# Low halves of the weights, the last norm's factors and v's copies: which engine does them in the second block

## The chip, the cores and the metric

The kernel runs on one core of a Trainium2 chip. The metric is the device time of one execution in microseconds (us). A core has five engines that run side by side, each through its own queue in order: TensorE (PE in the rows; PEld is its loading of weights), VectorE (DVE), ScalarE (ACT), GpSimd (POOL) and SyncE (SP, which here only issues the transfers from HBM).

## The reference

Two blocks on 256 tokens of width 1024. The first is two hybrid attention layers with an MLP and a norm at the end; the second is one layer with a modulation, two mixers and 16 experts. What matters here:

```python
x = first_block(...)                       # ends in rms_norm(x, norm_final)
h_l = modulate(rmsnorm(x, norm1), sh1, sc1)      # latents
h_c = modulate(rmsnorm(ctx, norm1), sh1c, sc1c)  # context
# mixer: both through w_in (columns for q, kv, rope, x_m, z and two gates)
x_c = silu(dwconv(x_m, conv_w, conv_b))          # five taps
q, k, v = blockdiag(x_c, w_q), blockdiag(x_c, w_k), blockdiag(x_m, w_v)
# MLA attention of the latents over context and latents, and an mLSTM over both
x = x + g1 * ((sigmoid(g_mla) * y_mla + sigmoid(g_ml) * y_ml) @ w_out)
x = x + g2 * ec_moe(modulate(rmsnorm(x, norm2), sh2, sc2))   # 16 experts, 201 MB of weights
return rmsnorm(x, final_norm)
```

## The kernel before

Activations lie with features on partitions: `xT` is 8 tiles of 128 features by 256 tokens. A float32 product is made of three fast ones (`three`): both operands are split into a high half (the value rounded to float32r) and a low half (what the rounding leaves), and high times high, high times low and low times high are summed in PSUM. Weights come by `load_w` into four buffers `wr` and are split piece by piece in the generator `pieces` (512 columns each): ScalarE casts the high half (`A.copy`, L352), then `src - high` gives the low half, on VectorE (L358) or, for the share of pieces that `share[0]` sets, on GpSimd (L356). In the second block there are four places for pieces, so ScalarE and VectorE can be up to four pieces ahead of TensorE; a piece of a `w_stationary` product is 12 matmuls of 256 columns.

TensorE's order is written out by hand in the program. The other engines' orders are made by the scheduler of the framework when the program is built, from the dependences and the priorities that the code gives (`tc.high_priority`); each engine then runs its queue in that order, and an instruction that waits holds up all behind it.

The first block and its second MLP end near 771 us of the profiled execution. The second block then goes through these stages:

- **Context** (771 to 842 us). Four products `xm`, then the features (`ml_features`): per feature tile k, `conv` makes `pre` (one operation on ScalarE, L1125, four scalar_tensor_tensor on VectorE, L1127), its tanh `cth` on ScalarE and `xcc` on VectorE (L1131). `products(f)` for f = 0, 2, 4, 6 makes v (`per_token`, eight matmuls into `bd`, copied by L1160 into `vex`) and k (`per_feature`, from `xcc`, copied by ScalarE, L1164, into `kT`), and the gates. The tiles `bd` of v come from the pool `accp` with two banks, of which the gates' sum `og` holds one, so v's product for f + 2 waits for the copy of f. Beside it run keys and values of the context (`keys_values`: `kvl`, `kn`, `v`), the norm at the end of the first block and the latents' modulation (`modt`, L975, and `hx`, L981 and L982).
- **Latents** (842 to 889 us): the same features for the latents (`xh` is their `xc`).
- **mLSTM** (889 to 960 us), with gate products (`tanh`) between its steps.
- **Readout, keys, values and queries of the latents** (960 to 1012 us).
- **Attention and output product** (1012 to 1108 us).
- **Routing and experts** (1108 us to the end). Expert weights are loaded into buffers that the stages before leave free, in one queue on SP.

`share[0]` was set to 0.34 in the context and latents stages and to 0.2 after them (`SH1`, `SH2`, `SH3`); in the second MLP it is 0.2 (`SHM`) and the MLP leaves it at `SH0`, which is 0.

The norm at the end of the first block isn't applied to `xT` at once: its factors (gain `g_fin` per feature, `rb1` per token) go into the modulation, and at the end of the context stage `xT` itself is multiplied by both, in two operations for each k:

```python
for k in range(8):
    A.activation(xT[:, k], xT[:, k], AF.Copy, scale=vc("g_fin", k))     # L1660
    G.tensor_tensor(xT[:, k], xT[:, k], rb1, op=OP.mult)                # L1661
```

Of the kernel before, what the change touches and what calls it, by code (L numbers as in the profile page):

```python
# [10 lines left out]
AF = mybir.ActivationFunctionType  # L11
OP = mybir.AluOpType
# [32 lines left out]
TAIL = 4  # L45
HP = 40
SH0 = 0.0
SH1 = (0.34, 0.34, 0.34)
SH2 = 0.34
SH3 = 0.2  # L50
NG = 1
FX = (2.0, 5.0, 1.0, 4.0)
FL = 2.0
# [188 lines left out]
def fused_kernel(ctx: ExitStack, tc: tile.TileContext, I, out):  # L242
    nc = tc.nc
    V, A, G, PE = nc.vector, nc.scalar, nc.gpsimd, nc.tensor
# [24 lines left out]
    xT = per.tile([128, 8, 256], FT, name="xT")  # L269
# [17 lines left out]
    def vc(n, j=0, w=1):  # L287
        o = vcols[n][0] + j
        return vbuf[:, o:o + w]
# [35 lines left out]
    share = [0.0, 0.0]  # L325
# [790 lines left out]
    def ml_features(xs, xc, kT, vex, gp, wg, tp):  # L1116


        xm = tp.tile([128, 8, 260], FT, tag="xm", name="xm")
        V.memset(xm[:, :, 0:2], 0.0)  # L1120
        V.memset(xm[:, :, 258:260], 0.0)
        def conv(j):
            for k in (2 * j, 2 * j + 1):
                pre = tp.tile([128, 256], FT, tag="pre", name="pre", bufs=2)
                A.activation(pre, xm[:, k, 0:256], AF.Identity, scale=vc("cw", k), bias=vc("cb", k))  # L1125
                for w in range(1, 5):
                    V.scalar_tensor_tensor(pre, xm[:, k, w:w + 256], vc("cw", w * 8 + k), pre, op0=OP.mult,  # L1127
                                           op1=OP.add)
                th = tp.tile([128, 256], FT, tag="cth", name="cth", bufs=2)
                A.activation(th, pre, AF.Tanh, scale=0.5)  # L1130
                V.scalar_tensor_tensor(xc[:, k], th, 1.0, pre, op0=OP.add, op1=OP.mult)  # L1131

        for j in range(4):
            o = fl_tile("xm")
            yield from w_stationary(load_w(I["w_in2"][j]), xs, o)
            A.copy(xm[:, 2 * j:2 * j + 2, 2:258], pair(o))
            if CV[j] is not None:
                conv(CV[j])
            yield None
        og = acc_tile("gt")  # L1140

        def per_token(o, n, src, f):
            for j in range(2):
                b = bds[:, 8 * n + f + j]
                for t in range(2):
                    c0 = t * 256 + j * 128
                    mm(o[:, c0:c0 + 128], src[:, f + j, t * 128:(t + 1) * 128], b, j == 0 and t == 0, True)

        def per_feature(o, n, f):
            for j in range(2):  # L1150
                mm(o[:, j * 256:(j + 1) * 256], bds[:, 8 * n + f + j], xc[:, f + j], j == 0, True)

        def tokens(o):
            return o[:, 0:512].rearrange("p (t n) -> p t n", t=2)

        def products(f):
            o = acc_tile("bd")
            per_token(o, 0, xm[:, :, 2:258], f)
            with tc.high_priority(offset=HQ):
                V.tensor_copy(vex[:, :, f // 2], tokens(o))  # L1160
            o = fl_tile("bd")
            per_feature(o, 1, f)
            with tc.high_priority(offset=HQ):
                A.activation(kT[:, f:f + 2], pair(o), AF.Copy, scale=1.0 / 64)  # L1164
            for j in range(2):
                for i, rhs in enumerate((xc[:, f + j], xm[:, f + j, 2:258])):
                    g = 2 * j + i
                    mm(og[32 * g:32 * g + 32, 0:256], wg[:, i * 8 + f + j], rhs, f == 0, f == 6)

        for f in (0, 2, 4, 6):  # L1170
            products(f)
            if CV[4 + f // 2] is not None:
                conv(CV[4 + f // 2])
            yield 2.6
            yield None
        A.copy(gp[-1], og[:, 0:256])
# [419 lines left out]
    vex = [mx_.tile([128, 2, 4, 256], FT, name=f"vex{s}") for s in range(2)]  # L1596
# [7 lines left out]
    with ExitStack() as es:  # L1604
        fp = pool(es, "b2c")
        xcc = fp.tile([128, 8, 256], FT, name="xcc")

        def ctx_path():
            yield from in_turn(ml_features(cx, xcc, kTc, vex[0], gp, wg, fp),
                               keys_values(0, cx, kn[0], vt[0], kp0, fp))  # L1610

        share[0] = SH1[0]
        cg = F.add(ctx_path())

        s1 = fp.tile([128, 256], FT, name="s1")
        s2 = fp.tile([128, 256], FT, name="s2")
        for k in updated(dn):
            for s_, sc, eng in ((s1, 1.0, G), (s2, vc("g_fin", k), V)):
                d = s_ if k == 0 else fp.tile([128, 256], FT, tag="sqf", name="sq", bufs=3)
                A.activation(d, xT[:, k], AF.Square, scale=sc)  # L1620
                if k:
                    eng.tensor_tensor(s_, s_, d, op=OP.add)
            F.fill(FX[2])
        share[0] = SH1[1]
        scg = fp.tile([128, 32], FT, name="scg")[:, 0:8]
        V.tensor_tensor(scg, sc1[:, 0], vc("g_fin", 0, 8), op=OP.mult)
        F.fill(FX[0])
        r1 = rstd_cols(s1, 1024, "fin")
        ps = acc_tile("ps_s2")
        for t in range(2):  # L1630
            mm(ps[:, t:t + 1], s2[:, t * 128:(t + 1) * 128], ones[:, 0:1], t == 0, True)
        r2 = fp.tile([128, 2], FT, name="r2")
        V.scalar_tensor_tensor(r2, ps[:, 0:2], 1.0 / 1024, r1, op0=OP.mult, op1=OP.mult)
        V.tensor_tensor(r2, r2, r1, op=OP.mult)
        V.tensor_scalar(r2, r2, EPS, None, op0=OP.add)
        G.tensor_tensor(r2, r2, mhalf[:, 0:2], op=OP.pow)
        V.tensor_tensor(r2, r2, r1, op=OP.mult)
        F.fill(FX[1])
        rb2 = fp.tile([128, 256], FT, name="rb2")
        bcast_rows(r2, rb2)  # L1640
        rb1 = fp.tile([128, 256], FT, name="rb1")
        bcast_rows(r1, rb1)
        for _ in modulated(xT, rb2, scg, modT[:, 0, 0:8], fp, into(hh, hl)):
            F.fill(FX[3])
        share[0] = SH1[2]
        F.need(cg)

        sh2 = modT[:, 0, 24:32]
        ss = per.tile([128, 8], FT, name="ssh")
        lb0 = per.tile([128, 16], FT, name="lb0")  # L1650
        lb_ps = fl_tile("lb0")
        sw = fp.tile([128, 8, 16], FT, name="sw")
        V.tensor_tensor(sw, vc("wrt", 0, 128).rearrange("p (k e) -> p k e", k=8),
                        sh2[:, :, None].to_broadcast([128, 8, 16]), op=OP.mult)
        sws = fp.tile([128, 16], FT, name="sws")
        V.tensor_reduce(sws, sw.rearrange("p k e -> p e k"), axis=AX.X, op=OP.add)
        mm(lb_ps[:, 0:16], ones, sws, True, True)
        V.tensor_copy(lb0, lb_ps[:, 0:16])
        for k in range(8):
            A.activation(xT[:, k], xT[:, k], AF.Copy, scale=vc("g_fin", k))  # L1660
            G.tensor_tensor(xT[:, k], xT[:, k], rb1, op=OP.mult)  # L1661
    xh_ = x2p.tile([128, 2, 2048], FT, tag="xh", name="xh")
    xc = xh_[:, 0].rearrange("p (k n) -> p k n", k=8)
    hm = xh_[:, 1].rearrange("p (t n) -> p t n", t=2)
# [2 lines left out]
    with ExitStack() as es:  # L1667
        qp_ = pool(es, "b2q")
        kT = qp_.tile([128, 8, 256], FT, name="kT")
        ca = qp_.tile([128, 8, 256], FT, name="ca")  # L1670
        share[0] = SH2
        gates = [tanh_pair(7 + 8 * i + j, xs, tzg[i][:, 2 * j:2 * j + 2]) for j in range(4) for i in range(2)]
        with ExitStack() as e2:
            mlf = ml_features(xs, xc, kT, vex[1], gp, wg, pool(e2, "b2f"))

            def context_gates():
                gates_per_token(gp[0], gt[0])
                gp.append(mx_.tile([128, 256], FT, tag="gp", name="gp1"))
                yield from log_gates(gt[0], gc[0], mx_)
                for _ in range(NL):  # L1680
                    yield None
                yield from context_rows(gc[0], ca)

            drain(in_turn(mlf, context_gates(), *gates[:NG]))
        share[0] = SH3
        for g in gates[NG:]:
            F.add(g)
        F.fill(FG)
        gates_per_token(gp[1], gt[1])
        lg = log_gates(gt[1], gc[1], mx_)  # L1690
        next(lg)
        next(lg)
        F.fill(FL)
        drain(lg)
        with ExitStack() as e2:
            mlstm(xc, kT, ca, hm, ss, pool(e2, "b2m"))
        F.fill(1e9)
# [71 lines left out]
    for j in range(4):  # L1769
# [3 lines left out]
        o = os2[j]  # L1773
        drain(po[j])
        for i in range(2):
            k = 2 * j + i
            V.scalar_tensor_tensor(xT[:, k], o[:, i * 256:(i + 1) * 256], modT[:, 0, 16 + k:17 + k], xT[:, k],
                                   op0=OP.mult, op1=OP.add)
# [14 lines left out]
    for t in range(2):  # L1793
        V.scalar_tensor_tensor(lb[:, t], lg[:, 256 + t * 16:256 + (t + 1) * 16], rc[:, t:t + 1], lb0, op0=OP.mult,
                               op1=OP.add)
# [77 lines left out]
    for d in range(9):  # L1873
        if d < 8:
            o = acc_tile("xs")[:, 0:128]
# [160 lines left out]
```

## Time and profile before

| | |
|---|---|
| median of three runs | 1550.09 us (1548.2 to 1552.66) |
| the profiled execution | 1552.58 us, of which the span from first to last instruction is 1550.8 us |
| busy share of the span | PE 87%, PEld 72%, DVE 59%, ACT 43%, POOL 16% |
| read from HBM | 402.08 MB, 260 GB/s over the span |

A busy share is a mean over stages with different limits, so the rows below are taken by stage. "Idle before" and "waited for" name the instruction whose end released the waiting one. The granted clock (PEclk) is a share of TensorE's full speed.

### The profile page before, as it was taken

How to read it: one execution, taken by the hardware profiler on the slowest of the kernel's cores; microseconds unless marked ns; L12 is line 12 of the kernel's file. 1: busy time of each engine (PE TensorE's matmuls, PEld its weight loads, DVE VectorE, ACT ScalarE, POOL GpSimd, SP SyncE). 2: the span in 40 equal slices, each digit the busy share in tenths (PEclk: the TensorE clock that was granted, in tenths of full speed). 3: DMA queues.
4: the chain of work that ended last, by engine and by line, in shares of the span. 5: the costliest groups of instructions: out<-in, count | busy, mean ns of one | idle time of the engine just before them, and what ended most of it. 6: DMA issues, size and time to landing. Idle time of an engine off the chain costs nothing. (4 is left out here: it accounts for less than half of the span.)

```text
span 1550.8 us, 27054 instructions
## 1 busy us (share of the span) xinstructions
PE 1353.3 (87%) x10903; PEld 1117.5 (72%) x10903; DVE 913.0 (59%) x1615; ACT 662.4 (43%) x1341; POOL 241.9 (16%) x204
## 2 busy tenths in 40 slices
PE   8999999999999999999988999999798565656565
PEld 7999989999999999999987899989542111111114
DVE  8986788877887689899897775965410000000001
ACT  7566555555557556455566566554210000000001
POOL 3100022221210026433252111310100000000000
PEclk9999999999999999999999999999899877887878
DMA  8544447766453456768843322555799999999997
GB/s 323 201 142 156 169 141 280 259 251 233 161 185 133 155 204 253 284 254 312 318 164 109 109 82 89 205 203 195 321 382 427 427 430 427 429 428 429 427 429 316
DMA packets 50557, 404.87 MB, mean 261 GB/s; under 512 B 5504, under 2 KB 7424, under 8 KB 14464
## 3 DMA queue, kind: packets, MB, share of 16 engines
q1 hardware_dynamic: 50288, 403.04, 67.0%
q8 instruction: 85, 1.39, 0.4%
q14 instruction: 40, 0.33, 0.1%
q10 hardware_dynamic: 144, 0.11, 0.0%
HBM read 402.08 MB, written 1.05 MB: 260 GB/s over the span
## 5 line engine op out<-in xcount | busy, mean ns | idle before, releaser
L352 ACT CAST wh<-wr 128x512 fp32r<-128x512 f32 (+1 forms) x647 | 386.0, 615 | 265.7 <-PE gate L295 45.8
L358 DVE TENSOR_TENSOR wh<-wr,wh 128x512 fp32r<-128x512 f32 (+1 forms) x563 | 417.6, 756 | 112.9 <-ACT wh L352 109.2
L295 PE MATMUL up<-hx,wh 128*128 128x256 f32 x1536 | 185.5, 278 | 6.2 <-DVE wh L358 2.7
L356 POOL TENSOR_TENSOR wh<-wr,wh 128x512 fp32r<-128x512 f32 (+1 forms) x84 | 123.1, 1465 | 427.7 <-ACT wh L352 378.4
L295 PEld LDWEIGHTS up<-hx,wh 128*128 128x128 f32 x1536 | 179.1, 188 | 9.2 <-DVE wh L358 4.1
L295 PE MATMUL dn<-ux,wh 128*128 128x256 f32 x1536 | 180.0, 277 | 0.4 <-POOL wh L356 0.4
L295 PEld LDWEIGHTS dn<-ux,wh 128*128 128x128 f32 x1536 | 177.1, 188 | 0.8 <-POOL wh L356 0.6
L1954 DVE TENSOR_TENSOR ew<-up,ew 128x512 f32<-128x512 f32 x8 | 5.5, 692 | 245.9 <-PE up L295 245.9
L295 PE MATMUL gate<-hx,wh 128*128 128x256 f32 x1152 | 135.5, 278 | 0.0
L295 PEld LDWEIGHTS gate<-hx,wh 128*128 128x128 f32 x1152 | 133.1, 188 | 1.4 <-issue 1.4
L295 PE MATMUL y<-ew 128*32 128x128 f32 (+1 forms) x896 | 78.1, 499 | 46.1 <-DMA ew<-in_w_e_down_dram 45.4
L295 PE MATMUL up<-ew,xsr 128*32 128x512 f32 x384 | 66.9, 831 | 49.2 <-DMA ew<-in_w_e_up_dram 49.2
L295 PE MATMUL gate<-ew,xsr 128*32 128x512 f32 x384 | 60.9, 763 | 46.0 <-DMA ew<-in_w_e_gate_dram 46.0
L295 PEld LDWEIGHTS y<-ew 128*32 128x32 f32 x896 | 28.7, 123 | 92.2 <-DMA ew<-in_w_e_down_dram 51.9
L1948 ACT ACTIVATE ew<-gate 128x512 f32<-128x512 f32 x8 | 4.8, 597 | 210.2 <-PE gate L295 208.9
L295 PEld LDWEIGHTS up<-ew,xsr 128*32 128x32 f32 x384 | 12.4, 132 | 104.4 <-DMA ew<-in_w_e_up_dram 71.8
L295 PEld LDWEIGHTS gate<-ew,xsr 128*32 128x32 f32 x384 | 11.9, 124 | 93.7 <-DMA ew<-in_w_e_gate_dram 62.9
L295 PE MATMUL tanh<-hx,wh 128*128 128x256 f32 x576 | 75.9, 284 | 0.3 <-DVE wh L358 0.2
L295 PE MATMUL z<-hx,wh 128*128 128x256 f32 x576 | 71.8, 282 | 4.2 <-ACT wh L352 1.2
L295 PEld LDWEIGHTS z<-hx,wh 128*128 128x128 f32 x576 | 68.3, 188 | 6.8 <-DVE hx L433 1.6
L295 PEld LDWEIGHTS tanh<-hx,wh 128*128 128x128 f32 x576 | 70.4, 188 | 1.4 <-DVE wh L358 0.7
L1925 DVE SCALAR_TENSOR_TENSOR ew<-y,gsl,xT 128x512 f32<-128x512 f32 (+2 forms) x10 | 6.4, 644 | 107.1 <-PE y L295 107.0
(451 smaller groups left out, 2039.6 us busy)
## 6 DMA issues: line engine op xcount, KB each, us to landing
ew<-in_w_e_up_dram SPq DMA_DIRECT2D x26, 2048.0 KB, 21.7
ew<-in_w_e_down_dram SPq DMA_DIRECT2D x25, 2048.0 KB, 21.1
ew<-in_w_e_gate_dram SPq DMA_DIRECT2D x24, 2048.0 KB, 21.7
wr<-in_w_up_dram SPq DMA_DIRECT2D x32, 1024.0 KB, 4.9
wr<-in_w_down_dram SPq DMA_DIRECT2D x32, 1024.0 KB, 5.3
wr<-in_w_gates_dram SPq DMA_DIRECT2D x24, 1024.0 KB, 4.8
wr<-in_w_modT_dram SPq DMA_DIRECT2D x24, 1024.0 KB, 5.0
wr<-in_w_in_dram SPq DMA_DIRECT2D x24, 1024.0 KB, 4.8
```

The source lines that it names most:

```text
L295: PE.matmul(o, l, r, start=st, stop=sp, skip_group_check=True)
L352: A.copy(hv, src)
L356: behind[1] = G.tensor_tensor(lv, src, hv.bitcast(FT), op=OP.subtract).ins
L358: behind[0] = V.tensor_tensor(lv, src, hv.bitcast(FT), op=OP.subtract).ins
L1925: V.scalar_tensor_tensor(dst[:, c0:c0 + w], src, gsl[:, G4:G4 + 1], rows[:, 0, c0:c0 + w], op0=OP.mult, op1=OP.mult)
L1948: A.activation(h[:, j * 512:(j + 1) * 512], gate[j], AF.Silu)
L1954: V.tensor_tensor(h[:, c], up[j], h[:, c], op=OP.mult)
```

## The change

Three edits, all in the second block. The low halves of all weight pieces are made on VectorE (`share` stays 0). The last norm's two factors are applied to `xT` in one VectorE operation for each k, in place of one on ScalarE and one on GpSimd. The copies of v's products into `vex` are made on ScalarE in place of VectorE.

```diff
-SH1 = (0.34, 0.34, 0.34)
-SH2 = 0.34
-SH3 = 0.2
...
             o = acc_tile("bd")
             per_token(o, 0, xm[:, :, 2:258], f)
             with tc.high_priority(offset=HQ):
-                V.tensor_copy(vex[:, :, f // 2], tokens(o))
+                A.copy(vex[:, :, f // 2], tokens(o))
...
-        share[0] = SH1[0]
...
-        share[0] = SH1[1]
...
-        share[0] = SH1[2]
...
         for k in range(8):
-            A.activation(xT[:, k], xT[:, k], AF.Copy, scale=vc("g_fin", k))
-            G.tensor_tensor(xT[:, k], xT[:, k], rb1, op=OP.mult)
+            V.scalar_tensor_tensor(xT[:, k], xT[:, k], vc("g_fin", k), rb1, op0=OP.mult, op1=OP.mult)
...
-        share[0] = SH2
...
-        share[0] = SH3
```

TensorE's and SyncE's orders stay as they were, row for row. VectorE has 599 low halves where it had 563, and GpSimd 48 where it had 84: 36 pieces move, 12 of them in the context stage, 6 with the latents, 5 in the mLSTM, 7 in the readout stage and 6 in the attention stage.

On VectorE the end of the context stage stood in this order (`xcc` is the convolved context, `lb` a small row that TensorE makes after the stage's last product, and the `wh` behind it are low halves for the latents):

```order
L1131 SCALAR_TENSOR_TENSOR xcc<-cth,pre 128x256
L975 SCALAR_TENSOR_TENSOR modt<-xT,scg,rb_9396 128x256
L358 TENSOR_TENSOR wh<-wr,wh 128x512
L1160 COPY vex_9089<-bd 128x2x256
L1131 SCALAR_TENSOR_TENSOR xcc<-cth,pre 128x256
L982 SCALAR_TENSOR_TENSOR hx<-modt,modT,hx 128x256
L1160 COPY vex_9089<-bd 128x2x256
L358 TENSOR_TENSOR wh<-wr,wh 128x512
L1160 COPY vex_9089<-bd 128x2x256
L1658 COPY lb_9811<-lb_9812 128x16
```

The same place of VectorE's queue in the changed kernel (line numbers are three to six lower there):

```order
L1124 SCALAR_TENSOR_TENSOR pre<-xm,vbuf,pre 128x256 x8
L979 SCALAR_TENSOR_TENSOR hx<-modt,modT,hx 128x256
L972 SCALAR_TENSOR_TENSOR modt<-xT,scg,rb_9396 128x256
L1128 SCALAR_TENSOR_TENSOR xcc<-cth,pre 128x256 x2
L355 TENSOR_TENSOR wh<-wr,wh 128x512
L979 SCALAR_TENSOR_TENSOR hx<-modt,modT,hx 128x256
L1654 SCALAR_TENSOR_TENSOR xT<-xT,vbuf,rb_9401 128x256 x5
L1652 COPY lb_9811<-lb_9812 128x16
L1654 SCALAR_TENSOR_TENSOR xT<-xT,vbuf,rb_9401 128x256 x3
L355 TENSOR_TENSOR wh<-wr,wh 128x512
```

The copies into `vex` have left the queue, and the eight operations on `xT` stand behind the last `xcc`, around `lb` and ahead of the third low half for the latents.

On ScalarE the second half of the context's features stood so before (`vt` is the context's value tile, `cth` the tanh of the convolution):

```order
L1130 ACTIVATE cth<-pre 128x256
L1023 ACTIVATE vt_6908<-v,rc_kv 128x256
L1023 ACTIVATE vt_6910<-v,rc_kv 128x256
L1023 ACTIVATE vt_6908<-v,rc_kv 128x256
L1023 ACTIVATE vt_6910<-v,rc_kv 128x256
L1130 ACTIVATE cth<-pre 128x256
L981 ACTIVATE hx<-modt,modT 128x256
L1164 ACTIVATE kTc<-bd 128x512
L1660 ACTIVATE xT<-xT,vbuf 128x256
```

And so it stands in the changed kernel:

```order
L1020 ACTIVATE vt_6910<-v,rc_kv 128x256
L1157 COPY vex_9089<-bd 128x2x256
L1020 ACTIVATE vt_6908<-v,rc_kv 128x256
L1161 ACTIVATE kTc<-bd 128x512
L1020 ACTIVATE vt_6910<-v,rc_kv 128x256
L1127 ACTIVATE cth<-pre 128x256 x2
L1157 COPY vex_9089<-bd 128x2x256
L978 ACTIVATE hx<-modt,modT 128x256
L1161 ACTIVATE kTc<-bd 128x512
```

The copy for f = 2 (the first `vex` here) stands among the value copies, ahead of the last convolution's two tanhs, and the copy for f = 4 right behind them; the operations on `xT` are gone.

## Rows read from the trace of the kernel before

**Rows 1.** Busy time of each engine by stage: us, busy us (instructions), PEclk, DMA share, GB/s.
```profile
771.00:842.00 71.00, 60.97 (x453) 54.49 (x452) 62.59 (x110) 45.33 (x100) 31.22 (x29) 0.95 0.44 160
842.00:889.00 47.00, 44.12 (x348) 39.87 (x348) 35.21 (x72) 27.73 (x53) 8.15 (x6) 0.93 0.31 113
...
960.00:1012.00 52.00, 49.23 (x390) 46.95 (x389) 46.95 (x97) 31.07 (x67) 18.05 (x15) 1.00 0.51 185
1012.00:1108.00 96.00, 94.73 (x672) 86.60 (x671) 51.92 (x96) 43.20 (x86) 7.71 (x6) 1.00 0.64 245
```
**Rows 2.** Waits of TensorE from 771 to 1108 us: total us, times, longest.
```profile
PE bd L295 <- DVE vex L1160: 6.9, 2, 4.0
PE uq L295 <- DVE wh L358: 2.0, 2, 1.5
PE xm L295 <- DVE wh L358: 2.0, 2, 1.3
```
**Rows 3.** Busy time in short stretches, columns as in rows 1.
```profile
834.40:838.00 3.60, 3.50 (x12) 2.72 (x12) 2.07 (x5) 0.78 (x2) 1.01 (x1) 0.54 0.02 5
876.50:882.00 5.50, 5.50 (x24) 3.82 (x25) 4.54 (x13) 1.95 (x4) 0.00 (x0) 0.50 0.52 191
```
**Rows 4.** Timeline around one GpSimd piece: start us, us, engine, line, operation.
```profile
819.90 2.71 DVE L1127 SCALAR_TENSOR_TENSOR pre<-xm,vbuf,pre 128x256 f32<-128x256 f32 x4
...
820.40 1.53 POOL L356 TENSOR_TENSOR wh<-wr,wh 128x512 fp32r<-128x512 f32 x1 [0.97 <-ACT wh L352]
...
823.14 1.66 DVE L1127 SCALAR_TENSOR_TENSOR pre<-xm,vbuf,pre 128x256 f32<-128x256 f32 x4
```
**Rows 5.** VectorE's timeline later in the stage, columns as in rows 4.
```profile
815.22 2.47 DVE L1014 TENSOR_TENSOR kn<-kn,rkb 128x512 f32<-128x512 f32 x4
...
834.37 0.41 DVE L1131 SCALAR_TENSOR_TENSOR xcc<-cth,pre 128x256 f32<-128x256 f32 x1
```
**Rows 6.** VectorE's groups by shape, 772 to 842 us: busy us, mean ns, idle before.
```profile
L1127 DVE SCALAR_TENSOR_TENSOR pre<-xm,vbuf,pre 128x256 f32<-128x256 f32 x32 | 20.4, 666 | 0.1
L358 DVE TENSOR_TENSOR wh<-wr,wh 128x512 fp32r<-128x512 f32 x20 | 16.9, 847 | 0.7 <-POOL s L1622 0.7
L982 DVE SCALAR_TENSOR_TENSOR hx<-modt,modT,hx 128x256 fp32r<-128x256 f32 x8 | 5.8, 725 | 0.0
...
L975 DVE SCALAR_TENSOR_TENSOR modt<-xT,scg,rb 128x256 f32<-128x256 f32 x8 | 3.7, 476 | 0.0
L1160 DVE COPY vex<-bd 128x512 f32<-128x512 f32 x4 | 2.7, 686 | 3.4 <-PE bd L295 3.4
```
**Rows 7.** GpSimd's groups by shape, 764 to 842 us.
```profile
L356 POOL TENSOR_TENSOR wh<-wr,wh 128x512 fp32r<-128x512 f32 x12 | 17.4, 1447 | 15.9 <-ACT wh L352 15.9
L1661 POOL TENSOR_TENSOR xT<-xT,rb 128x256 f32<-128x256 f32 x8 | 7.2, 899 | 16.0 <-ACT xT L1660 13.5 <-PE kn L295 2.4
```
**Rows 8.** ScalarE's group of k copies out of PSUM, 772 to 842 us.
```profile
L1164 ACT ACTIVATE kTc<-bd 128x512 f32<-128x512 f32 x4 | 2.4, 594 | 4.9 <-PE bd L295 4.9
```
**Rows 9.** VectorE's groups by shape: the first of 842 to 890 us, the second of 960 to 1012 us.
```profile
L1127 DVE SCALAR_TENSOR_TENSOR pre<-xm,vbuf,pre 128x256 f32<-128x256 f32 x32 | 18.5, 605 | 1.0 <-ACT pre L1125 0.6
...
L358 DVE TENSOR_TENSOR wh<-wr,wh 128x512 fp32r<-128x512 f32 x21 | 16.4, 791 | 1.5 <-ACT wh L352 1.3
```
**Rows 10.** The chain that ended last, in order of time: start us, us, what.
```profile
1025.51 2.94 PE scl L295 x16
...
1118.95 425.62 issue
```
**Rows 11.** Expert stage: busy time as in rows 1, and SP's timeline (start us, us).
```profile
1140.00:1545.00 405.00, 260.23 (x1960) 79.24 (x1952) 21.50 (x39) 18.11 (x39) 0.39 (x1) 0.83 0.99 420
...
1124.97 8.33 SPq L1509 DMA_DIRECT2D ew<-in_w_e_up_dram  x5
```
**Rows 12.** TensorE's timeline where the context stage ends, columns as in rows 4.
```profile
834.50 1.92 PE L295 MATMUL bd<-bds,xm 128*128 128x128 f32 x8 [3.99 <-DVE vex L1160]
...
841.40 5.90 PE L295 MATMUL xm<-hx,wh 128*128 128x256 f32 x48
```

## The prediction

> **What bounds the kernel now.** I first read the stages [rows 1]. From 771 to 1108 us TensorE has most of the work, and what it doesn't use is what a change elsewhere can win: 71.0 - 61.0 = 10.0 us idle in the context stage, 47.0 - 44.1 = 2.9 with the latents, 52.0 - 49.2 = 2.8 in the readout stage, 96.0 - 94.7 = 1.3 in the attention. VectorE is the engine to look at: busy 62.6 of 71 us in the context stage and 47.0 of 52 in the readout stage, but only 35.2 of 47 and 51.9 of 96 in the two others. The waits agree [rows 2]: TensorE's longest are for VectorE, 6.9 us in two waits for the copies into `vex` and twice 2.0 us for low halves. Each `vex` wait also costs TensorE speed [rows 3]: after standing for 4.0 us [rows 12] it runs 834.4 to 838 us at a granted clock of 0.54, mostly its lower level of 1.2 GHz, which loses 0.46 x 3.6 = 1.7 us; after the other it runs 876.5 to 882 us at 0.50, all at 1.2 GHz, which loses 2.75 us.
>
> Then I asked why VectorE is so busy. One place shows it [rows 4]. Four `pre` operations take 1.66 us together when GpSimd is idle, and 2.71 us when a low half of 1.53 us on GpSimd begins among them: 1.05 us more for the same work. The groups say the same of the whole stage [rows 6]: `pre` has a mean of 666 ns and `hx` of 725, where `modt`, of the same operation and shape, has 476; `wh` has 847 ns, where the undisturbed price of a 128x512 operation with two inputs is near 676 (the four `kn` [rows 5] take 2.47 us, 0.62 from one to the next and some 0.06 more for a single one). So a VectorE operation on two SBUF inputs stands still while GpSimd works, and a piece that GpSimd takes over costs VectorE about as much as, or more than, making it itself.
>
> **The change part by part, context stage.** VectorE's time until the last `xcc` decides here, since the last two products of `products` need it.
>
> - Blocked time, before: `pre` 32 x (0.666 - 0.476) = 6.1 us, `wh` 20 x (0.847 - 0.676) = 3.4, `hx` 8 x (0.725 - 0.476) = 2.0; together 11.5. GpSimd loses its 12 pieces of 1.45 us and its 8 `xT` operations of 0.90 [rows 7]; seven additions for the norm stay, so I take 10.5 as gone (bounds 7 and 11.5).
> - Added: 12 low halves, of which one lies before 771 us under the MLP. 11 x 0.62 = 6.8 us.
> - Removed: the two `vex` copies ahead of the last `xcc`, 2 x 0.69 = 1.4 us [rows 6].
>
> The last `xcc` comes 10.5 - 6.8 + 1.4 = 5.1 us earlier. Behind it TensorE now needs 841.4 - 834.8 = 6.6 us to the end of the stage [rows 5, 12], because f = 4 had been held up by the `vex` copy of f = 2 and ran at the lower clock. With the copy on ScalarE, right behind the product, f = 4 can run before the last `xcc`, and only f = 6 is left behind it, which saves about 4.1 us: the stretch from 834.5 to 838.0 [rows 3, 12] and some 0.6 us of gate products behind it, an estimate. That makes 9.2; TensorE can't give more than its 10.0 us of idle time and 1.7 of clock, and VectorE will now and then wait for a tanh from ScalarE. I take **9 us** (4 to 11.7).
>
> Costed at nothing: the four `vex` copies on ScalarE. The nearest row is the copy of k out of PSUM of the same size, 594 ns [rows 8], and ScalarE is busy only 45.3 of 71 us and loses eight operations on `xT`; if that cover is gone, each holds up v's next product by 0.6, 2.4 us in all. Also at nothing: the eight operations on `xT`, at the price of four such operations in a row, 1.66 us [rows 4], 8 x 0.42 = 3.4 us. They stand behind the last `xcc`, around the wait for `lb`, and ahead of the third low half for the latents. What hides them are the first two pieces of the latents' product, which are split before and keep TensorE for 24 matmuls of the 48 that take 5.90 us [rows 12], so 2.95 us, and the product of f = 6. Without that cover it is up to 3.4 us.
>
> **Latents.** Blocked: `pre` 32 x (0.605 - 0.476) = 4.1 us [rows 9]. Added: 6 x 0.62 = 3.7. Removed ahead of the last `xh`: three `vex` copies, 2.1. So VectorE is through 2.5 us earlier. The wait for the first `vex` copy, 2.9 us, had VectorE's backlog of convolution ahead of the copy; it goes when ScalarE copies, and with it some or all of the 2.75 us of clock. The two overlap, so I take **3.5 us** of the at most 5.6 (low end 1).
>
> **Readout, mLSTM, attention.** In the readout stage `wh` has 791 ns, so 21 x 0.115 = 2.4 us blocked there alone, and the shuffled rotations lose too; seven added low halves cost 4.3. The four products on GpSimd for the rotations stay. I take **0** (2.8 gained, which is all the idle time, to 2 lost). In mLSTM and attention VectorE has room and TensorE waits for almost nothing: 0, within 1 either way.
>
> The sum is 9 + 3.5 = 12.5 us. It is taken from the profiled execution, 1552.58 us, of which 1.8 lie outside the span: 1540.1. That execution was 2.5 us above the median of 1550.09, which so becomes 1537.6; I say 1537.5.
>
> Does it reach the end? The chain that ended last runs through TensorE's attention up to 1119 us and then shows 426 us without a named step [rows 10], in which the DMA engines are 99% busy at 420 GB/s [rows 11]. The stream of expert weights sets the end, but its start is tied to the stages before: SP's queue issues at 1124.97 us [rows 11], after the routing, loads into buffers that the stages before had held. If these stages end earlier, the stream moves with them, so I count the gain in full.
>
> **The rivals.** A gain that is mostly taken back: VectorE remains the bound of the context stage and only its own shortening counts, 5.1 us there, less 1 for the readout stage, and 2.5 with the latents; the tail of 4.1 us stays, since on ScalarE the copy for f = 4 stands behind two tanhs that wait for VectorE. For it: VectorE is still nearly full. Against it: the copy for f = 2, the one that was waited for, stands ahead of them. 6.6 us, **1543.5**.
>
> No change, because the stream of expert weights sets the end and doesn't move: 1550. For it: 420 GB/s over 405 us. Against it: the issue at 1124.97 us, and the chain through TensorE. It would need the loads up to there to be late by themselves; the DMA engines are at 0.64 in the stage before [rows 1].
>
> Slower: the long VectorE operations are not GpSimd's doing, or the rest of GpSimd's work causes them. Then VectorE, full already, only gets more: in the context stage 6.8 + 3.4 - 4 x 0.69 = +7.5 us, with the latents 3.7 - 2.8 = +0.9, in the readout stage +4.3, together 12.7, **1563**. It decides as soon as less than 12.7 of the 18.0 us that I count as blocked (11.5 + 4.1 + 2.4) goes away, by VectorE's time alone. Against it are the two `pre` rows beside each other, 2.71 and 1.66.
> The Trainium skill (Perfetto Trace Analysis, Optimizing Scalar/DVE Operations) has a rule on that side: when VectorE is saturated, giving work to ScalarE or even GpSimd may make sense. By that the low halves should stay where they are, and the sum would be the +12.7 us just worked out; the page adds that VectorE and GpSimd share a read port, so that moving work between them may not help, and the trace, with 1.05 us lost by VectorE to one piece of 1.53, is on the side of the addition.
>
> **How the numbers follow.** A difference under 0.3%, 4.7 us, can't be told from no change. Forecast, 5 to 18 us gained: 0.62, its own range 1532 to 1545. Taken back: 0.18, of which a quarter falls within 0.3%. A gain beyond the forecast, up to the 17 us idle and 4.4 of clock: 0.03. Lost in the stream: 0.07. Slower: 0.10. Faster is then 0.62 + 0.135 + 0.03, less a little for the forecast's own lower edge, 0.77; slower 0.10; the rest, 0.13, is the same. The range goes from 1530 (20 us, near all that TensorE has to give) to 1547, which takes in the gain that is taken back and leaves out most of the no change and the slower case.
>
> **What the profile after would show.** If the blocking is right, `pre`, `wh` and `hx` in the context stage come down to near 480, 690 and 480 ns, and VectorE is busy for less or the same time there in spite of 19 more operations on weights and `xT`. If the `vex` step is right, the 6.9 us of waits of `bd` fall to under 2, ScalarE's copies take about 0.6 us, and both stretches at 1.2 GHz are gone or short. If the cover of `xT` is right, TensorE starts the latents' `xm` without a wait over 0.5 us. If the gain reaches the end, the time from the routing's last step to the end is unchanged within 2 us. The prediction is wrong if the means of VectorE's groups stay up, if a new wait of TensorE for ScalarE's tanh or copy stands where `vex` stood, or if low halves make it wait over 4 us in the readout stage.

## The result and the profile after

The changed kernel takes 1533.43 us (median of 4 runs, 1533.25 to 1534.38), beside 1551.24 us for the kernel before (median of 4, 1548.2 to 1552.66). The ratio is 0.9883, with a 95% interval of 0.987 to 0.9896: 17.8 us or 1.2% faster. The forecast was 1537.5 us, so the direction and the range held, and the gain was larger than the 12.5 us worked out. The profiled execution took 1534.38 us, with a span of 1532.6.

The stages of the changed kernel, in the order and with the columns of [rows 1] (window, its length, busy us of TensorE's matmuls, its weight loads, VectorE, ScalarE and GpSimd, granted clock, DMA share, GB/s):

```profile
771.00:829.70 58.70, 56.83 (x447) 52.32 (x446) 54.13 (x118) 44.34 (x96) 8.98 (x10) 0.97 0.48 172
829.70:871.00 41.30, 41.30 (x350) 38.18 (x350) 34.00 (x81) 29.51 (x57) 0.00 (x0) 1.00 0.45 154
...
942.50:994.00 51.50, 48.89 (x390) 47.50 (x389) 46.61 (x104) 31.87 (x68) 8.52 (x8) 0.99 0.52 187
994.00:1089.00 95.00, 95.00 (x671) 87.30 (x670) 54.99 (x101) 42.46 (x85) 0.00 (x0) 0.99 0.65 247
```

The first two rows hold the gain. TensorE stood idle for 10.0 us of the context stage; now it is 1.9. With the latents it now works all the time. VectorE's busy time in the context stage fell from 62.6 to 54.1 us, though VectorE got more to do. Marked by TensorE's landmarks, the first product with `xh` (771.7 before, 771.5 after), the first of the latents (841.4, 829.7), the last gate product (888.5, 870.8), the first `kvl` (963.7, 946.3), the first `scl` (1011.9, 994.1), the last `xtok` product (1107.8, 1089.0) and the span's end (1550.8, 1532.6), the change is 11.5 us gained in the context stage, 6.0 with the latents, 0.3 lost in the mLSTM, 0.4 gained in the readout stage, 1.0 in the attention, 0.6 lost from there to the end.

TensorE's waits of the changed kernel from 771 us on that lie in these stages, columns as in [rows 2]:

```profile
PE uq L292 <- DVE wh L355: 2.6, 2, 1.8
PE ps_kv L292 <- DVE rb L475: 1.9, 1, 1.9
PE arow L296 <- DVE gc L1203: 1.0, 1, 1.0
```

Neither `bd` nor `xm` waits any more. Where TensorE had run at its lower level of 1.2 GHz [rows 3], the corresponding stretches now have the full clock:

```profile
822.00:826.00 4.00, 4.00 (x32) 3.14 (x31) 4.00 (x11) 3.95 (x10) 0.00 (x0) 1.00 0.02 4
862.00:871.00 9.00, 9.00 (x77) 6.68 (x75) 6.23 (x18) 5.54 (x12) 0.00 (x0) 1.00 0.33 118
```

One stretch at the lower level, which the prediction didn't count, stays: 798 to 801 us at a granted clock of 0.50, where the kernel before has 801 to 804 us at 0.50.

VectorE's groups of the context stage, 772 to 830 us, as in [rows 6]:

```profile
L355 DVE TENSOR_TENSOR wh<-wr,wh 128x512 fp32r<-128x512 f32 x30 | 21.2, 714 | 2.0 <-ACT wh L349 2.0
L1124 DVE SCALAR_TENSOR_TENSOR pre<-xm,vbuf,pre 128x256 f32<-128x256 f32 x32 | 14.3, 482 | 0.1
L1618 DVE TENSOR_TENSOR s<-s,sq 128x256 f32<-128x256 f32 x7 | 4.2, 599 | 0.1
L979 DVE SCALAR_TENSOR_TENSOR hx<-modt,modT,hx 128x256 fp32r<-128x256 f32 x8 | 3.8, 483 | 0.0
...
L1128 DVE SCALAR_TENSOR_TENSOR xcc<-cth,pre 128x256 f32<-128x256 f32 x8 | 3.2, 423 | 0.0
```

Same operations, same shapes: `pre` went from 666 to 482 ns, `hx` from 725 to 483, `wh` from 847 to 714. And the end of the stage on VectorE, columns as in [rows 4]:

```profile
825.42 0.76 DVE L1128 SCALAR_TENSOR_TENSOR xcc<-cth,pre 128x256 f32<-128x256 f32 x2
826.09 0.69 DVE L355 TENSOR_TENSOR wh<-wr,wh 128x512 fp32r<-128x512 f32 x1
826.69 0.49 DVE L979 SCALAR_TENSOR_TENSOR hx<-modt,modT,hx 128x256 fp32r<-128x256 f32 x1
827.09 2.07 DVE L1654 SCALAR_TENSOR_TENSOR xT<-xT,vbuf,rb 128x256 f32<-128x256 f32 x5
829.84 0.17 DVE L1652 COPY lb<-lb 128x16 f32<-128x16 f32 x1 [0.69 <-PE lb L292]
```

with TensorE beside it:

```profile
826.89 1.16 PE L292 MATMUL bd<-bds,xm 128*128 128x128 f32 x8
827.88 1.03 PE L292 MATMUL bd<-xcc,bds 128*128 128x256 f32 x4
...
829.41 0.39 PE L292 MATMUL lb<-sws,cbuf 128*128 128x16 f32 x2
829.66 5.90 PE L292 MATMUL xm<-hx,wh 128*128 128x256 f32 x48
```

The last `xcc` ends at 825.42 + 0.76 = 826.2 us, where it ended at 834.8 [rows 5]; the latents' product follows 3.5 us later, where it took 6.6, and it starts right behind `lb`, without a wait. The chain that ended last still runs over TensorE up to the routing and ends in a stretch of the same length as in [rows 10]:

```profile
1080.47 5.85 PE wo L292 x48
1100.24 426.16 issue
```

### The profile page after: what moved, and what is told of

It reads as the page before. It is cut to its first block, busy times and chain, and to the rows that moved or that the text cites. A ratio compares the mean times of both kernels' runs of the same rounds, so it can differ in the third digit from the quotient of the medians.

```text
span 1532.6 us, 27005 instructions
## 1 busy us (share of the span) xinstructions
PE 1343.5 (88%) x10903; PEld 1116.7 (73%) x10903; DVE 908.9 (59%) x1651; ACT 663.4 (43%) x1341; POOL 188.2 (12%) x160
## 4 chain that ended last, share of the span: by engine, by line
PE 63%; issue 29%; DVE 6%; ACT 1%; POOL 0%; DMA 0%; SPq 0%; POOLq 0%; ACTq 0%; DVEq 0%
PE dn L292 13%; PE up L292 9%; PE gate L292 9%; PE z L292 4%; PE tanh L292 4%; PE xm L292 3%; PE v L292 3%; PE prj L292 2%; DVE wh L355 2%; PE wo L292 2%; PE scl L292 1%; PE sc L292 1%; PE bd L292 1%; PE S L292 1%; PE pvl L292 1%
## 5 line engine op out<-in xcount | busy, mean ns | idle before, releaser
L355 DVE TENSOR_TENSOR wh<-wr,wh 128x512 fp32r<-128x512 f32 (+1 forms) x599 | 440.3, 749 | 110.2 <-ACT wh L349 107.2
L353 POOL TENSOR_TENSOR wh<-wr,wh 128x512 fp32r<-128x512 f32 x48 | 74.5, 1551 | 210.1 <-ACT wh L349 178.8
```

Source lines behind the costliest of these rows:

```text
L353: behind[1] = G.tensor_tensor(lv, src, hv.bitcast(FT), op=OP.subtract).ins
L355: behind[0] = V.tensor_tensor(lv, src, hv.bitcast(FT), op=OP.subtract).ins
```

## The experiments

In the expectations, A is the prediction's account: a VectorE operation on SBUF stands still while GpSimd works, so a low half that GpSimd makes costs VectorE at least what making it would. By rival Q the gain comes from the copies into `vex`, which stand in VectorE's queue; by rival L a piece that GpSimd makes only comes late to TensorE. Both give the low halves alone under 5 us, and L gives repeating GpSimd's pieces almost nothing. All ratios are to the kernel before, with 95% intervals behind them.

**Each edit alone.** The low halves alone:

```diff
-SH1 = (0.34, 0.34, 0.34)
-SH2 = 0.34
-SH3 = 0.2
+SH1 = (0.0, 0.0, 0.0)
+SH2 = 0.0
+SH3 = 0.0
```

> Only the low halves move to VectorE; copies into vex and the two operations on xT stay as before. Theory A (GpSimd's work blocks VectorE, the moved pieces are what frees it): 9 to 13 us faster than before, pre in the context stage falls from a mean of 666 ns to under 560, and the vex waits of TensorE fall too, since VectorE's backlog is shorter. Rival Q (the gain comes from the vex copies standing in VectorE's queue): under 5 us faster, the 6.9 us of vex waits stay above 5. Rival L (a piece on GpSimd only comes late to TensorE, 1.45 against 0.68 us): 1 to 3 us faster, pre stays near 666 ns.

Measured: 1534.64 us, ratio 0.9895 (0.9878 to 0.9912), 17.5 us faster. That is nearly the whole change, more than A said and out of reach of both rivals. VectorE's means fall although the copies into `vex` are still there:

```profile
L358 DVE TENSOR_TENSOR wh<-wr,wh 128x512 fp32r<-128x512 f32 x31 | 21.6, 705 | 1.6 <-ACT wh L352 1.6
L1127 DVE SCALAR_TENSOR_TENSOR pre<-xm,vbuf,pre 128x256 f32<-128x256 f32 x32 | 15.1, 486 | 0.1
...
L1160 DVE COPY vex<-bd 128x512 f32<-128x512 f32 x4 | 2.7, 672 | 0.0
```

and TensorE's wait for them has shrunk from 6.9 us to 0.3; it waits 1.3 us for `xcc` in their place.

The copies alone:

```diff
-                V.tensor_copy(vex[:, :, f // 2], tokens(o))
+                A.copy(vex[:, :, f // 2], tokens(o))
```

> Only the copies into vex move to ScalarE. Theory A: 4 to 7 us faster: the vex waits go, but VectorE stays blocked (pre near 650 ns) and the last xcc comes as late as before, so that TensorE waits for it. Rival Q: 10 to 13 us faster, nearly all of the change's 17.8 us with the latents' part. Rival L: 4 to 7 us as well.

Measured: 1545.22 us, 0.9956 (0.9938 to 0.9973), 6.9 us faster. That is within A's range and L's, and out of Q's. `pre` stays at 667 ns, but TensorE doesn't wait for the last `xcc`, which A had expected. Half of its wait for `vex` is left, and it is for ScalarE now:

```profile
PE bd L295 <- ACT vex L1160: 3.4, 2, 2.0
```

The last norm's factors alone:

```diff
-            A.activation(xT[:, k], xT[:, k], AF.Copy, scale=vc("g_fin", k))
-            G.tensor_tensor(xT[:, k], xT[:, k], rb1, op=OP.mult)
+            V.scalar_tensor_tensor(xT[:, k], xT[:, k], vc("g_fin", k), rb1, op0=OP.mult, op1=OP.mult)
```

> Only the norm's factors move: one VectorE operation for each k in place of one on ScalarE and one on GpSimd. Theory A: 0 to 3 us faster, since eight GpSimd operations of 0.9 us fewer block VectorE by up to 5 us in the context stage while 3.4 us are added at its end. Rivals Q and L: 0 to 3.4 us slower, by the added operations on the fullest engine.

Measured: 1548.47 us (10 runs), 0.9975 (0.9965 to 0.9984), 3.6 us faster, a little over what A gave. `hx`, which GpSimd's eight operations on `xT` had met, falls to 473 ns; `pre` stays at 666. The profiled execution, at 1545.92 us the second fastest of the ten, shows one thing more. In its latents the longest wait for `vex` is as long as before, and yet the clock is full:

```profile
PE bd L295 <- DVE vex L1160: 2.9, 1, 2.9
836.50:880.70 44.20, 41.33 (x347) 38.28 (x350) 35.72 (x75) 27.36 (x53) 8.19 (x6) 1.00 0.40 144
```

So the stretch at 1.2 GHz that followed this wait in the kernel before [rows 3] doesn't come with the wait alone.

**Each edit undone in the changed kernel.** First the copies into `vex` back on VectorE, the other two edits kept (the diff of the copies above, reversed):

> The changed kernel with the copies into vex back on VectorE. Theory A: 12 to 15 us faster than before, so at most 5 us lost to the changed kernel, and vex waits of 1 to 3 us. Rival Q: under 6 us faster than before.

Measured: 1532.91 us, 0.9882 (0.9866 to 0.9899), the same as the changed kernel and better than the 12 to 15 us that A gave. The waits of 1 to 3 us for `vex` that A expected aren't there. All of TensorE's waits in it from 771 to 1000 us:

```profile
PE uq L295 <- DVE wh L358: 2.4, 2, 1.6
PE ps_kv L295 <- DVE rb L478: 1.8, 1, 1.8
PE arow L299 <- DVE gc L1206: 1.0, 1, 1.0
PE tanh L295 <- DVE wh L358: 0.8, 1, 0.8
```

No `vex` among them, with the copies on VectorE at 688 ns each. The clock is 1.00 in 822 to 826 and 862 to 871 us here too. Once VectorE has no backlog, the place of these copies makes no difference that these runs can tell.

Then the factors for `xT` back on ScalarE and GpSimd (the diff of the factors, reversed):

> The changed kernel with the norm's factors back on ScalarE and GpSimd. Theory A (GpSimd's reading work blocks VectorE): 16 to 19 us faster than before, since the low halves alone already gave 17.5. A rival (the xT operations' share of the blocking is needed too): 10 to 14 us faster.

Measured: 1535.11 us, 0.9895 (0.988 to 0.991), 1.7 above the changed kernel, with overlapping intervals; it is within A's range and out of the rival's. The loss is small, but its mark is plain. GpSimd's group, and VectorE's two groups that now run beside it:

```profile
L1661 POOL TENSOR_TENSOR xT<-xT,rb 128x256 f32<-128x256 f32 x8 | 10.2, 1290 | 22.4 <-ACT xT L1660 22.4
```
```profile
L982 DVE SCALAR_TENSOR_TENSOR hx<-modt,modT,hx 128x256 fp32r<-128x256 f32 x8 | 4.7, 594 | 0.0
L975 DVE SCALAR_TENSOR_TENSOR modt<-xT,scg,rb 128x256 f32<-128x256 f32 x8 | 4.7, 593 | 0.0
```

GpSimd's own operation has grown from 899 ns [rows 7] to 1290, so the blocking seems to go both ways. Which of VectorE's operations hold it up, no run isolates.

Last the low halves back on GpSimd, the two other edits kept (`SH1`, `SH2` and `SH3` as before):

> The changed kernel with the shares of the low halves back on GpSimd. Theory A: 7 to 11 us faster than before, the sum of the two edits alone (6.9 and 3.6) at most. Rival Q: 13 us faster or more, as the two edits would support each other.

Measured: 1542.54 us, 0.994 (0.9924 to 0.9957), half of the gain and within A's range. `pre` is at 668 ns again and `wh` at 745; TensorE waits 3.2 us for `vex`, now on ScalarE. In its window with the latents TensorE waits 1.4 us for `vex` where it had waited 2.9:

```profile
836.00:882.00 46.00, 44.61 (x379) 41.06 (x373) 33.22 (x75) 30.76 (x61) 8.15 (x6) 1.00 0.36 135
```

The clock is full there, without the stretch at 1.2 GHz of [rows 3]. That can't be put down to the copies on ScalarE, since the clock is full with the factors alone too, where the copies are on VectorE.

**The blocking by itself.** The changed kernel, whose low halves all come from VectorE, with GpSimd repeating 17 of them (context stage and latents) into a tile that nobody reads:

```diff
                     else:
                         behind[0] = V.tensor_tensor(lv, src, hv.bitcast(FT), op=OP.subtract).ins
+                    if twin and twins[0]:
+                        d = spare[0][:, :sz].rearrange("p (k n) -> p k n", k=k1 - k0)
+                        G.tensor_tensor(d, src, hv.bitcast(FT), op=OP.subtract)
```

> The changed kernel, in which GpSimd repeats every low half that it made before in the context and latents stages, into a spare tile that nobody reads (17 extra subtractions; the one that TensorE uses is made on VectorE). Theory A: 6 to 14 us slower than the changed kernel, so 4 to 12 us faster than before, and pre in the context stage is back above 600 ns. Rival L (a piece made on GpSimd only comes late): within 2 us of the changed kernel, pre near 480 ns.

Measured: 1543.57 us, 0.9948 (0.9933 to 0.9963), 10.1 us above the changed kernel. Nothing that is needed depends on the added work, so its cost is contention or the holding of input buffers. The holding is small: SP waits for these pieces three times, 3.4 us in all, but in the context stage VectorE waits only 0.5 us for ScalarE's high halves, and no wait of ScalarE of 0.3 us or more is for a load. VectorE and GpSimd in the context stage:

```profile
L362 DVE TENSOR_TENSOR wh<-wr,wh 128x512 fp32r<-128x512 f32 x30 | 25.2, 845 | 0.5 <-ACT wh L354 0.5
L1134 DVE SCALAR_TENSOR_TENSOR pre<-xm,vbuf,pre 128x256 f32<-128x256 f32 x32 | 16.2, 536 | 0.1
L1631 DVE TENSOR_TENSOR s<-s,sq 128x256 f32<-128x256 f32 x7 | 5.5, 780 | 0.1
L989 DVE SCALAR_TENSOR_TENSOR hx<-modt,modT,hx 128x256 fp32r<-128x256 f32 x8 | 4.8, 606 | 0.0
```
```profile
L365 POOL TENSOR_TENSOR spare<-wr,wh 128x512 f32<-128x512 f32 x11 | 17.4, 1582 | 31.2 <-ACT wh L354 23.3 <-issue 7.9
```

The same VectorE operations are longer by 30 x 131 + 32 x 54 + 7 x 181 + 8 x 123 ns = 7.9 us beside 11 pieces, 0.72 us a piece, and two small operations add 1.6 us. TensorE's context stage, by the landmarks, is 65.5 us long where it was 58.2, so 7.3 longer, which is about what VectorE lost. `pre` came to only 536 ns, where over 600 was expected: the block falls on whatever runs beside the piece, here mostly on `wh`.

The same place in the program, but GpSimd only fills the tile with zeros (`G.memset(d, 0.0)` in place of the last line of the diff):

> As the run before, but GpSimd only fills the spare tile with zeros, 17 times, and reads nothing for it. If reading by GpSimd is what blocks VectorE: within 2 us of the changed kernel, pre near 480 ns. If any work of GpSimd on its memory blocks VectorE: 4 us slower than the changed kernel or more, pre above 550 ns.

Measured: 1535.51 us, 0.9895 (0.988 to 0.991), 2.1 above the changed kernel, with overlapping intervals.

```profile
L365 POOL MEMSET spare<- 128x512 f32 x12 | 6.3, 525 | 31.9 <-ACT kTc L1171 31.5
```
```profile
L362 DVE TENSOR_TENSOR wh<-wr,wh 128x512 fp32r<-128x512 f32 x31 | 21.6, 702 | 2.1 <-ACT wh L354 2.1
L1134 DVE SCALAR_TENSOR_TENSOR pre<-xm,vbuf,pre 128x256 f32<-128x256 f32 x32 | 14.2, 479 | 0.1
L1631 DVE TENSOR_TENSOR s<-s,sq 128x256 f32<-128x256 f32 x7 | 5.4, 765 | 0.1
```

`wh` and `pre` stay short; only `s` grows, by 166 ns. The fills are 6.3 us of GpSimd's time against 17.4, and the last of them ran at the stage's end, so the time alone doesn't settle whether fills block. The timeline does for these fills, with GpSimd's own additions `s`, which read, as the comparison. Each pair of fills lies between two additions, so its place is sure:

```profile
775.01 0.75 POOL L1631 TENSOR_TENSOR s<-s,sq 128x256 f32<-128x256 f32 x1
775.08 0.96 DVE L1631 TENSOR_TENSOR s<-s,sq 128x256 f32<-128x256 f32 x1
775.70 1.11 POOL L365 MEMSET spare<- 128x512 f32 x2
776.25 0.68 DVE L362 TENSOR_TENSOR wh<-wr,wh 128x512 fp32r<-128x512 f32 x1
```

VectorE's `s` beside GpSimd's reading takes 0.96 us, where others of the group take 0.41. The low half beside two fills takes 0.68, its undisturbed time, and so do the ones that start beside fills at 774.27 and 777.73. The mean of `s` has grown by GpSimd's additions, which met VectorE's at other moments than in the changed kernel.

**Once more, and further.** The changed kernel again, and the changed kernel with the MLPs' 48 remaining low halves on VectorE too, with the additions of the norm's first sum on VectorE, and with both.

> The changed kernel once more (the shares written as 0), as the yardstick for the three runs beside it: 17 to 19 us faster than before.

Measured: 1533.52 us, 0.9878 (0.9864 to 0.9893): 19.1 us faster, at the upper edge of what was expected.

```diff
-SHM = (0.2, 0.2)
+SHM = (0.0, 0.0)
...
-            with tc.issue_after(behind[1]):
+            with tc.issue_after(behind[0]):
```

(The last two lines stand in two places. They tie small preparations on GpSimd to VectorE's last low half, since GpSimd makes none any more.)

> The changed kernel with all low halves of both MLPs on VectorE as well (share 0 in place of 0.2; 48 pieces more). Theory A: the MLPs have TensorE busy nearly all the time and VectorE at about 85%, so there is little to win: within 3 us of the changed kernel, the wh mean of VectorE near 690 ns. A rival (VectorE is freed there as well, and its time was what TensorE waited for): 5 us faster or more. Another (VectorE becomes full there): 5 us slower or more.

Measured: 1533.03 us, 0.9873 (0.9856 to 0.9889): no difference to the changed kernel. In the second MLP `wh` falls from 834 ns (x103, the changed kernel's second run) to 720 (x127), so VectorE gains there too, but TensorE waits for little in that stage.

```diff
-            for s_, sc, eng in ((s1, 1.0, G), (s2, vc("g_fin", k), V)):
+            for s_, sc, eng in ((s1, 1.0, V), (s2, vc("g_fin", k), V)):
```

> The changed kernel with the seven additions for the first norm's sum on VectorE in place of GpSimd, the last reading work of GpSimd in the context stage. Theory A: the s group of VectorE falls from 600 to about 410 ns, seven additions of 0.33 us are added, together nearly nothing: within 2 us of the changed kernel. A rival (the rest of the blocking still costs TensorE its waits): 3 us faster or more.

Measured: 1531.39 us, 0.9864 (0.9849 to 0.9879), 2.1 below the changed kernel, too little to tell by time. In the trace the 14 additions take 420 ns each where the seven had 599, and the wait of `ps_kv` falls from 1.9 us to 0.2. The stretch at the lower clock from 798 to 801 us of the changed kernel is gone too: here 793 to 805 us have 1.00.

> Both of the last two edits on the changed kernel: within 4 us of it.

Measured: 1526.66 us (1526.42 to 1527.48), 0.9834 (0.9819 to 0.9848): 25.9 us below the kernel before and 6.9 below the changed one, so it beats both kernels. The expectation, within 4 us of the changed kernel, was wrong. In its context stage and with its latents TensorE has 0.2 us of idle time left and the full clock:

```profile
771.00:824.70 53.70, 53.52 (x432) 49.01 (x432) 52.53 (x125) 43.63 (x94) 3.01 (x3) 1.00 0.47 174
824.70:866.00 41.30, 41.30 (x351) 38.25 (x350) 33.71 (x81) 29.50 (x57) 0.00 (x0) 1.00 0.43 154
```

Between the first down product of the MLPs and the latents' first product the second run of the changed kernel takes 830.4 - 243.7 = 586.7 us, the kernel with the MLPs' pieces 828.5 - 243.7 = 584.8, that with the sums 828.3 - 244.8 = 583.5, and that with both 824.7 - 242.9 = 581.8. The first run of the changed kernel takes 829.7 - 243.2 = 586.5, so two executions of one kernel agree there within 0.2 us. In this stretch the two gains, 1.9 and 3.2 us, simply add (4.9 of 5.1). In the times of whole runs they are blurred by differences elsewhere: at that first product the profiled executions already differ by up to 1.9 us. Of the 7.2 us between the spans of the kernel with both and the second run of the changed one, 4.9 are these gains, 0.8 lie before 243 us and 1.5 behind the latents' start; where those two come from wasn't settled.

## Why the prediction was right, and where its sizes were off

**VectorE's blocked time: right, too small.** I took 10.5 of the 11.5 us of blocked time in three groups as gone. By the groups after, `pre` gives back 32 x 184 ns = 5.9 us, `wh` 20 x 133 = 2.7, `hx` 8 x 242 = 1.9: 10.5, as said. What the step left out are groups that I hadn't looked at: `xcc` fell from 539 to 423 ns (8, 0.9 us), `s` from 741 to 599 (7, 1.0 us), and one 2-column product for the norm's factor from 1.23 us to 0.16. These are 3.0 us more, all ahead of the last `xcc`, and they explain most of why it came 8.6 us earlier and not 5.1. The wrong term is the choice of groups: every VectorE operation of the stage should have been held against its undisturbed time. But the last `xcc` no longer decides the stage: with the copies back on VectorE it comes at 826.95 us, and the stage still takes 58.1 us, as in the changed kernel (58.2), where TensorE is busy for 56.8 of 58.7. The stage's 11.5 us, against the 9 forecast, are nearly the 11.7 that the forecast named as the most.

**The tail: size near, reason wrong.** The prediction gave 4.1 us, for the stretch behind the last `xcc`, to the copies on ScalarE. The tail did get 3.1 us shorter (6.6 to 3.5), and the wait and the 1.2 GHz stretch went. But with the copies back on VectorE all of this stays gone, and the copies alone shorten the context stage by only 1.3 us (69.7 to 68.4). What had held f = 4 up was VectorE's backlog ahead of the copy, and the low halves remove that by themselves. The copies' edit earns 6.9 us alone and nothing measurable on top of the others; that the term came out near its size is luck.

**Latents: 3.5 predicted, 6.0 measured, and 5.6 was named as the most.** All that there was came: TensorE is busy 41.3 of 41.3 us at clock 1.00. I had let the wait for `vex` and the lower clock overlap; they are one after the other, and both went. The ceiling was also a little low, since the clock of 0.50 lasts to 882.5 us: half of the 6.1 us that TensorE works at it is 3.0, and with 2.9 idle that makes 5.9. The tie that I made between the two, that each wait for `vex` costs clock, doesn't always hold: with the factors alone the same wait of 2.9 us stands there and the clock is 1.00. So only the idle part of the gain is shown to come from the wait that went. Why the clock fell there in the kernel before is open.

**Costed at nothing.** The eight operations on `xT` are hidden as said: five run beside f = 6, and the latents' product starts without a wait. ScalarE's copies have a median of 589 ns, beside the 594 taken from [rows 8].

**Readout, mLSTM, attention.** Readout 0, measured 0.4 gained: `wh` fell from 791 to 693 ns and the rotations' `rp` on two inputs from 742 to 414 (4), which pays for the seven added low halves (VectorE is busy 46.6 us, before 47.0), and the wait of `uq` went from 2.0 to 2.6 us, below the 4 that would have refuted it. The attention gained 1.0 that I hadn't counted; one wait of 1.1 us for ScalarE (`scl` for `pl`) is gone there. It stands in all four kernels in which GpSimd makes low halves in that stage and in none of the others, so it goes with them; how, no run looked into.

**The gain reaches the end: right.** From the last `xtok` product to the end it is 443.6 us, where it was 443.0.

**The rivals.** VectorE's time went down where the slower case had it go up by 7.5 us, and the twin shows why: GpSimd's piece costs VectorE time without giving anything. The stream of expert weights still sets the end, but that it doesn't move is excluded: the end came 18.2 us earlier. The gain that is mostly taken back comes nearest to the two kernels with the copies on ScalarE and the low halves on GpSimd: they gain 6.9 and 9.0 us, and TensorE waits 3.4 and 3.2 us for `vex` on ScalarE. In the changed kernel ScalarE makes the copy for f = 4 right behind the two tanhs, at 825.56 us, and TensorE doesn't wait for it.
The sum by the rule that a saturated VectorE should be relieved to GpSimd (the Trainium skill, Perfetto Trace Analysis, Optimizing Scalar/DVE Operations) has the wrong sign here; the page's remark on the shared port is what the runs bear out: the 36 low halves, moved onto the VectorE that was nearly full, gained 17.5 us.

**Adding up edits.** Alone they gain 17.5, 6.9 and 3.6 us, 28 together; the change gains 17.8. All three work against one thing, VectorE's backlog in the context stage and with the latents, and by the forecast's count TensorE had only 17 us idle and 4.4 of clock to give. With the latents this can be read stage by stage: in the profiled executions the low halves alone shorten it by 6.0 us, the copies alone by 4.5, the factors alone by 2.9, and all three together by 6.0. (The factors' 2.9 is the clock, and no run shows that this edit raises it.) The forecast treated two of them as separate terms of one sum and credited the tail and the latents to the copies; it came out low because VectorE's blocked time and the latents were sized low.

## What to carry to other kernels

A VectorE group whose mean is well above that of the same operation and shape elsewhere in the trace may be standing still, as here, and not be slow: look at what GpSimd does beside it, over all groups of the stage, and price a piece on GpSimd by what VectorE loses to it (0.72 us here beside a piece, while making it costs VectorE 0.62 to 0.69). When several edits relieve the same engine, bound their sum by what the engine that waits can still give, and don't assign one wait to one edit before trying each alone. Changes whose times alone can't be told from nothing can still be seen between landmarks of the trace, where two executions of one kernel agree (here within 0.2 us), and add up.

## What was not expected of the hardware

The blocking seems to be mutual and its amount depends on what meets: GpSimd's 128x256 operation took 899 ns on average before and 1290 where the low halves had moved to VectorE, and a product on only two columns on VectorE took 1.23 us beside a GpSimd piece and 0.16 without. VectorE's copies out of PSUM took the same time before and after (686 and 688 ns), but that says nothing of blocking, since GpSimd worked beside none of the eight in the trace before. One operation does say something: the sum of `xT` and a product in PSUM, with one input from SBUF, ran beside a GpSimd piece at 772.5 us of the kernel before and took no longer than the other 15 (673 to 689 ns). The next operation, on eight columns with both inputs in SBUF, took 0.70 us, and 0.15 in the changed kernel. And GpSimd's fills of a tile, which read nothing, ran beside three low halves without lengthening them.
